# Feed-forward tiles from 4 on all by seven products, in three groups of six

## The chip, the cores and the metric

The kernel runs on one core of a Trainium2 chip. TensorE (PE in the profile, its weight loads PEld) multiplies, VectorE (DVE), ScalarE (ACT) and GpSimd (POOL) compute elementwise, and SyncE (SP) issues the DMA transfers. The metric is device time in microseconds (us), the median of several executions.

## The reference, cut to what matters

Two layers, each with a feed-forward before and after a mixer (a pooling mixer in the first layer, attention in the second). So the feed-forward runs four times, each time with its own weights:

```python
def swiglu(h, w_gate, w_up, w_down):
    return (jax.nn.silu(h @ w_gate) * (h @ w_up)) @ w_down

h = rmsnorm(x, ffn_norm)             # x: 512 tokens x 1024 channels, float32
x = x + 0.5 * swiglu(h, w_gate, w_up, w_down)   # 2816 hidden channels
```

## The kernel before, in words

All is kept transposed: channels on the 128 partitions, the 512 tokens along the free dimension. x lies in SBUF as eight tiles of 128x512 (`xs`). The 2816 hidden channels make 22 tiles of 128. Every factor of a product is split into a high part in a reduced format (ScalarE, L117) and the remainder, the low part (VectorE, L118); `mm3` then takes three matmuls in place of one: high x high, high x low, low x high.

A **plain** product of one tile (`product`, L264) is 8 blocks of x (k) times three matmuls, 24 matmuls of 512 columns. A **pair by seven products** (`Two`, L364) computes two tiles of the same weight matrix as a 2 x 2 block product: the two tiles, the two halves of the 1024 input channels and the two halves of the 512 tokens are the blocks, and Strassen's method (in Winograd's form) needs seven block products in place of eight. Each is 4 k x 3 matmuls of 256 columns, so a pair is 84 matmuls of 256 columns, where two plain products are 48 of 512. For this it needs sums of the weight blocks (`w_sums`, L335: two loads into `raw`, four additions on VectorE at L350, and splits of the two tiles and of the sums, 3.5 of 1024 columns), sums of the blocks of x (`x_sums`, L321: for each of four k four subtractions of 256 columns at L327 and two splits of 512), and additions that put the products together (L434, with copies by ScalarE at L391). The seven products of a pair, by number: 1 uses a11, 6 uses s2, 5 uses s1, 3 uses s4, 7 uses s3, 2 uses a12, 4 uses a22. `twos` (L401) interleaves the products of consecutive pairs; the first pair begins with 1, 7, 6, 2.

A feed-forward (`ffn_in`, L258) goes through three groups of hidden tiles, `THIRDS`, 0 to 8, 8 to 16 and 16 to 22. A group first makes its hidden tiles `hs`, then the **down stage** (L500) multiplies them with w_down: for each of the eight output blocks m it loads the group's part of w_down[m] (`load_w`, L125, three buffers each of `raw`, `whi`, `wlo`), takes three matmuls of 512 columns for each hidden tile, and adds half the sum to `xs[m]` (L511 on VectorE).

In the first group tiles 0 to 3 are plain for gate and up, since the normalised x isn't there yet: they use x times the gain and scale the result by the row factors afterwards (`scaled`, L276). Meanwhile `normed` makes the normalised x and its split. Tiles 4 to 7 of the first group have a plain up product each, with `x_sums` of k = 0 to 3 after them one by one, and two pairs for the gate (L477 to L491). In the two later groups gate and up are both done by pairs.

Buffers that the parts share: `slot` (39 tiles of 128x512) holds the splits of x, of the normalised x, of its sums, and the hidden tiles; `t` (10 tiles) takes what `slot` doesn't; `work` has 6; `s` holds the sums of the weights and, before, two of the normalised blocks that `x_sums` reads. Each engine executes its own queue in order. The compiler of the kernel orders the queues ahead of the run, so an instruction may stand ahead of one that comes earlier in the program.

Of the kernel before, what the change touches and what calls it, by code (L numbers as in the profile page):

```python
# [9 lines left out]
F32 = mybir.dt.float32  # L10
F32R = mybir.dt.float32r
I32 = mybir.dt.int32
BF16 = mybir.dt.bfloat16
AF = mybir.ActivationFunctionType
# [4 lines left out]
P = 128  # L19
D = 1024  # L20
S = 512
FF = 2816
KD = D // P
NT = S // P
NFT = FF // P
THIRDS = ((0, 8), (8, 16), (16, 22))
WINDOWS = (2, 4, 8, 16)
H = 8
DN, DR = 128, 64
# [48 lines left out]
def trunk(ctx: ExitStack, tc: tile.TileContext, a: dict, out: bass.AP):  # L78
    nc = tc.nc
# [17 lines left out]
        return sp.tile(shape or [P, S], F32R, tag="slot", name="slot")  # L97

    def work(shape=None):
        return kp.tile(shape or [P, S], F32, tag="work", name="work", bufs=6)  # L100

    def small(n, dt=F32, tag=None, bufs=3):
        return tp.tile([P, n], dt, tag=tag or f"sm{n}", name="small", bufs=bufs)
# [4 lines left out]
    def mm3(ps, w, x, first, last):  # L108

        mm(ps, w[0], x[0], first, False)  # L110
        mm(ps, w[0], x[1], False, False)
        mm(ps, w[1], x[0], False, last)
# [145 lines left out]
    def ffn_in(fp, wg, wu, wd, prep, nxt, first, final):  # L258
# [2 lines left out]
        KH = KD // 2  # L261
        rows = None

        def product(w, x, turned=False, then=None):  # L264

            hi, lo = load_w(w, WC)
            p = acc()
            for i in range(KD):
                if then and i == KD - 4:
                    then()  # L270
                k = i % 2 * KH + i // 2 if turned else i
                ks = slice(k * P, (k + 1) * P)
                mm3(p, (hi[:, ks], lo[:, ks]), x[k], i == 0, i == KD - 1)
            return p

        def scaled(p):  # L276
# [13 lines left out]
        def halved(z, zu):  # L290
            nc.vector.tensor_mul(z, z, zu)
            h = slot(), slot()
            split(z, *h)
            return h
# [6 lines left out]
        xn, ts, kept = [None] * KD, {}, []  # L301

        def extra():
            return fp.tile([P, S], F32R, tag="t", name="t", bufs=10)

        def normed(k):

# [13 lines left out]
        def x_sums(k):  # L321

            b12, b11, b22, b21 = (kept[k][:, c * C : (c + 1) * C] for c in range(4))
            t = [work(), work()]
            t1, t2, t3, t4 = (x[:, c * C : (c + 1) * C] for x in t for c in range(2))
            for out, x, y in ((t1, b12, b11), (t2, b22, t1), (t3, b22, b12), (t4, b21, t2)):
                nc.vector.tensor_tensor(out=out, in0=x, in1=y, op=ALU.subtract)  # L327
            for e in range(2):
                new = extra if k < 2 else slot
                hi, lo = new(), new()  # L330
                split(t[e], hi, lo)
                ts[k, 2 * e] = hi[:, :C], lo[:, :C]
                ts[k, 2 * e + 1] = hi[:, C:], lo[:, C:]

        def w_sums(top, low):  # L335

            hw = WC // 2
            rt = wp.tile([P, WC], F32, tag="raw", name="raw")
            rl = wp.tile([P, WC], F32, tag="raw", name="raw")
            nc.sync.dma_start(rt, top)  # L340
            nc.sync.dma_start(rl, low)
            a11, a12, a21, a22 = rt[:, :hw], rt[:, hw:], rl[:, :hw], rl[:, hw:]
            s12 = fp.tile([P, WC], F32, tag="s", name="s", bufs=2)
            s34 = fp.tile([P, WC], F32, tag="s", name="s", bufs=2)
            s1, s2, s3, s4 = s12[:, :hw], s12[:, hw:], s34[:, :hw], s34[:, hw:]
            for out, x, y, op in (
                (s1, a21, a22, ALU.add), (s2, s1, a11, ALU.subtract),
                (s3, a11, a21, ALU.subtract), (s4, a12, s2, ALU.subtract),
            ):
                nc.vector.tensor_tensor(out=out, in0=x, in1=y, op=op)  # L350

            def halves(pool, src, n, tag, bufs=None):
                hi = pool.tile([P, n], F32R, tag=tag + "hi", name="hi", bufs=bufs)
                lo = pool.tile([P, n], F32R, tag=tag + "lo", name="lo", bufs=bufs)
                split(src, hi, lo)
                return [(hi[:, c : c + hw], lo[:, c : c + hw]) for c in range(0, n, hw)]

            a11, a12 = halves(wp, rt, WC, "w")
            s1, s2 = halves(wp, s12, WC, "w")
            s3, s4 = halves(fp, s34, WC, "c", 2)  # L360
            (a22,) = halves(fp, a22, hw, "d", 1)
            return a11, a12, a22, s1, s2, s3, s4

        class Two:  # L364
# [36 lines left out]
        def twos(todo):  # L401

            last = None
            for two in (*todo, None):
                if two:
                    two.load()
                if not last or not two:
                    one = last or two
                    for n in (5, 4, 3) if last else (1, 7, 6, 2):
                        one.product(n)  # L410
                else:
                    for one, n in (
                        (last, 5), (two, 1), (last, 4), (two, 7), (two, 6), (last, 3), (two, 2)
                    ):
                        one.product(n)
                if last:
                    yield last
                last = two

        def silu(two):  # L420
            nc.scalar.activation(two.z[:, :C], two.r, AF.Silu)
            nc.scalar.activation(two.z[:, C:], two.z[:, C:], AF.Silu)
            return two.z
# [24 lines left out]
                        last and k == KH - 1 and e == 2, skip=True,  # L448
                    )

        for f0, f1 in THIRDS:
            hs = []
            for f in range(f0, min(f1, 4), 2):
                if first and f == 0:
                    pg, pu = opening(wg[0], wu[0], prep)
                else:
                    pg = product(wg[f], xh)
                    if f == 2:
                        normed(0)
                    pu = product(wu[f], xh)  # L460
                    if f == 2:
                        normed(1)
                if rows is None:
                    r = prep.rstd()
                qg = product(wg[f + 1], xh)
                if rows is None:
                    rows = prep.rstd_rows(r)
                zs = scaled(pg), scaled(pu)
                if f == 2:
                    normed(2)  # L470
                hs.append(gated([(slice(0, S), zs[0])], zs[1]))
                qu = product(wu[f + 1], xh)
                zs = scaled(qg), scaled(qu)
                if f == 2:
                    normed(3)
                hs.append(gated([(slice(0, S), zs[0])], zs[1]))
            if f0 == 0:  # L477
                us, zu = [], None
                for e in range(4, 8):
                    u = product(wu[e], xn, e == 4)  # L480
                    if e < 6:
                        zu = zu if zu is not None else fp.tile([P, 2 * S], F32, tag="z", name="z", bufs=3)
                        z = zu[:, (e - 4) * S : (e - 3) * S]
                        nc.scalar.activation(z, u, AF.Copy)
                        u = z
                    us.append(u)
                    x_sums(e - 4)
                for e, gate in enumerate(twos([Two(wg, 4), Two(wg, 6)])):
                    z = silu(gate)
                    for i, u in enumerate(us[2 * e : 2 * e + 2]):  # L490
                        hs.append(halved(z[:, i * S : (i + 1) * S], u))  # L491
            else:
                z = None
                for e, two in enumerate(twos([Two(w, f) for f in range(f0, f1, 2) for w in (wg, wu)])):
                    if e % 2 == 0:
                        z = silu(two)
                    else:
                        times(z, two)
            nf = f1 - f0
            for m in range(KD):  # L500
                hi, lo = load_w(wd[m][:, f0 * P : f1 * P], nf * P)

                nc_ = 2 if final and f1 == NFT and m == KD - 1 else 1
                for e in range(nc_):
                    p = acc()
                    cs = slice(e * S // nc_, (e + 1) * S // nc_)
                    for f in range(nf):
                        fs = slice(f * P, (f + 1) * P)
                        h = hs[f][0][:, cs], hs[f][1][:, cs]
                        mm3(p[:, cs], (hi[:, fs], lo[:, fs]), h, f == 0, f == nf - 1)  # L510
                    nc.vector.scalar_tensor_tensor(  # L511
                        out=xs[m][:, cs], in0=p[:, cs], scalar=0.5, in1=xs[m][:, cs],
                        op0=ALU.mult, op1=ALU.add,
                    )
                    if final and f1 == NFT:
                        nc.sync.dma_start(out[m][:, cs], xs[m][:, cs])
                if f1 == NFT and not final:
                    nxt.add(m)
# [669 lines left out]
```

## Time and profile before

| | |
|---|---|
| time, median of 3 runs (lowest to highest) | 1672.87 us (1672.41 to 1673.0) |
| profiled execution | 1674.59 us, span 1672.8 us |
| TensorE, matmuls | 99% busy, 10246 matmuls, granted clock 0.998 |
| TensorE, weight loads | 89% |
| VectorE | 71% |
| ScalarE | 48% |
| GpSimd | 4% |
| DMA | 161.69 MB, mean 97 GB/s |

The span is the time from the first to the last instruction of one profiled execution; the execution's own time has about 1.8 us around it. A busy share is a mean over the span; the windows further below split it by stage. The second feed-forward (the one that most rows are from) lies between about 377 and 736 us, the four layers are alike.

### The profile page before, as it was taken

What the parts mean: (1) busy time and instruction counts of PE and PEld (TensorE: products, weight loads), DVE (VectorE), ACT (ScalarE), POOL (GpSimd) and SP (SyncE); (2) the same over time, 40 slices, a digit from 0 to 9 for tenths busy, and PEclk for the clock granted to TensorE, in tenths of its full rate; (3) what the DMA queues carried; (4) which work ended last, traced back from release to release, by engine and by line L of the source; (5) the groups of instructions that cost most, each with busy time, mean ns of one, the idle gap of its engine ahead of it and who ended that gap; (6) DMA issues with size and microseconds to landing.
All of it is one profiled execution on the core that took longest, in us unless ns stands there. A gap on an engine that the chain in (4) does not pass through costs nothing.

```text
span 1672.8 us, 25532 instructions
## 1 busy us (share of the span) xinstructions
PE 1659.1 (99%) x10246; PEld 1491.9 (89%) x10246; DVE 1182.8 (71%) x1940; ACT 800.7 (48%) x1347; POOL 69.7 (4%) x147
## 2 busy tenths in 40 slices
PE   8999999999999999999999999999999999999999
PEld 7889989987889989988899899888888788899898
DVE  8847847798757757668568567656778786586673
ACT  6534524454534525545445345446665454354351
POOL 0000000011000000000000000003321300000000
PEclk9999999999999999999999999999999999999999
DMA  5333333332332332333323323321112123233332
GB/s 179 101 101 101 102 103 99 97 112 77 109 105 85 118 105 89 98 101 96 107 89 103 112 89 108 103 88 52 45 57 89 59 82 111 89 102 114 89 110 91
DMA packets 48215, 161.69 MB, mean 97 GB/s; under 512 B 5728, under 2 KB 6496, under 8 KB 48096
## 3 DMA queue, kind: packets, MB, share of 16 engines
q1 hardware_dynamic: 47520, 159.34, 30.9%
q8 instruction: 80, 1.31, 0.3%
q10 hardware_dynamic: 576, 0.72, 0.1%
q14 instruction: 39, 0.32, 0.1%
HBM read 157.94 MB, written 2.10 MB: 96 GB/s over the span
## 4 chain that ended last, share of the span: by engine, by line
PE 97%; DVE 2%; ACT 1%; issue 0%; DMA 0%; POOL 0%; ACTq 0%; DVEq 0%; POOLq 0%
PE acc L106 95%; PE aux L702 1%; PE aux L106 1%; DVE slot L121 1%; PE aux L983 0%; DVE x L1018 0%; DVE wlo L118 0%; ACT work L964 0%; DMA gains<-in_gains 0%; DVE x L576 0%; ACT slot L117 0%; ACT slot L120 0%; ACT whi L117 0%; POOL work L969 0%; ACT work L852 0%
## 5 line engine op out<-in xcount | busy, mean ns | idle before, releaser
L106 PE MATMUL acc<-slot,whi 128*128 128x512 f32 x2428 | 752.4, 391 | 8.4 <-ACT whi L117 5.1
L106 PEld LDWEIGHTS acc<-slot,whi 128*128 128x128 f32 x2428 | 454.9, 189 | 102.8 <-ACT whi L117 5.6
L106 PE MATMUL acc<-slot,wlo 128*128 128x512 f32 (+1 forms) x1206 | 470.6, 390 | 0.0
L106 PE MATMUL acc<-slot,hi 128*128 128x256 f32 x2304 | 424.6, 281 | 0.1
L106 PEld LDWEIGHTS acc<-slot,hi 128*128 128x128 f32 x2304 | 356.9, 189 | 2.9 <-DVE z L434 1.9
L117 ACT ACTIVATE whi<-raw 128x1024 fp32r<-128x1024 f32 (+2 forms) x181 | 179.8, 996 | 333.8 <-PE acc L106 261.4
L106 PE MATMUL acc<-slot,lo 128*128 128x256 f32 x1152 | 324.3, 282 | 0.0
L106 PEld LDWEIGHTS acc<-slot,wlo 128*128 128x128 f32 x1206 | 227.7, 189 | 48.0 <-DVE wlo L118 1.3
L118 DVE TENSOR_TENSOR wlo<-raw,whi 128x1024 fp32r<-128x1024 f32 (+2 forms) x180 | 208.2, 1158 | 86.1 <-ACT whi L117 84.9
L106 PE MATMUL acc<-t,hi 128*128 128x256 f32 x1280 | 242.9, 282 | 0.0
L106 PEld LDWEIGHTS acc<-slot,lo 128*128 128x128 f32 x1152 | 218.4, 190 | 0.0
L118 DVE TENSOR_TENSOR lo<-s,hi 128x1024 fp32r<-128x1024 f32 x128 | 156.3, 1224 | 75.7 <-ACT hi L117 75.6
L117 ACT ACTIVATE hi<-s 128x1024 fp32r<-128x1024 f32 x128 | 135.1, 1058 | 139.9 <-PE acc L106 89.4
L106 PEld LDWEIGHTS acc<-t,hi 128*128 128x128 f32 x1280 | 196.7, 189 | 0.0
L106 PE MATMUL acc<-t,lo 128*128 128x256 f32 x640 | 181.1, 283 | 0.0
L511 DVE SCALAR_TENSOR_TENSOR x<-acc,x 128x512 f32<-128x512 f32 (+1 forms) x97 | 66.3, 684 | 136.9 <-PE acc L106 136.9
L117 ACT ACTIVATE hi<-raw 128x512 fp32r<-128x512 f32 (+1 forms) x128 | 107.9, 843 | 83.6 <-PE acc L106 65.6
L350 DVE TENSOR_TENSOR s<-raw 128x512 f32<-128x512 f32 x128 | 85.7, 688 | 70.8 <-DMA raw<-in_ffn_gate 62.7
L391 ACT ACTIVATE m<-acc 128x256 f32<-128x256 f32 x192 | 73.0, 381 | 109.1 <-PE acc L106 108.6
L118 DVE TENSOR_TENSOR lo<-raw,hi 128x512 fp32r<-128x512 f32 (+1 forms) x128 | 121.0, 953 | 0.0
L106 PEld LDWEIGHTS acc<-t,lo 128*128 128x128 f32 x640 | 120.5, 188 | 0.0
L106 PE MATMUL acc<-whi,slot 128*128 128x384 f32 (+2 forms) x320 | 87.6, 344 | 0.0
(191 smaller groups left out, 1472.0 us busy)
## 6 DMA issues: line engine op xcount, KB each, us to landing
raw<-in_ffn_gate SPq DMA_DIRECT2D x87, 512.0 KB, 3.5
raw<-in_ffn_up SPq DMA_DIRECT2D x87, 512.0 KB, 3.6
raw<-in_ffn_down SPq DMA_DIRECT2D x64, 512.0 KB, 3.5
raw<-in_ffn_down SPq DMA_DIRECT2D x32, 384.0 KB, 3.5
raw<-in_w_q SPq DMA_DIRECT2D x12, 384.0 KB, 3.2
raw<-in_w_in SPq DMA_DIRECT2D x8, 512.0 KB, 3.5
raw<-in_w_out SPq DMA_DIRECT2D x8, 512.0 KB, 3.6
x<-in_xT SPq DMA_DIRECT2D x8, 256.0 KB, 5.2
```

Source lines behind the costliest of these rows:

```text
L106: nc.tensor.matmul(ps, lhsT, rhs, start=start, stop=stop, skip_group_check=skip)
L117: nc.scalar.activation(hi, src, AF.Copy)
L118: nc.vector.tensor_tensor(out=lo, in0=src, in1=hi.bitcast(F32), op=ALU.subtract)
L121: nc.vector.scalar_tensor_tensor(out=lo, in0=src, scalar=scale, in1=hi.bitcast(F32), op0=ALU.mult, op1=ALU.subtract)
L350: nc.vector.tensor_tensor(out=out, in0=x, in1=y, op=op)
L391: nc.scalar.activation(self.kept[:, c[(1, 6, 7).index(n)]], part, AF.Copy)
L511: nc.vector.scalar_tensor_tensor(out=xs[m][:, cs], in0=p[:, cs], scalar=0.5, in1=xs[m][:, cs], op0=ALU.mult, op1=ALU.add,)
L702: nc.tensor.transpose(p[:, i * P : (i + 1) * P], src(i), ident)
```

## The change

`THIRDS` becomes `CHUNKS`, four groups: tiles 0 to 3, all plain, with a down stage of their own, and three groups of six tiles, all by pairs for gate and up. The four plain up products of tiles 4 to 7 fall away, with their copies; two more pairs are computed in a layer (18 in place of 16). `x_sums` moves into the down loop of the first group, one k ahead of each odd output block m. `work` gets 7 buffers, `t` 6 (only the sums of k = 0 and one block of x use it), and the split of a22 two.

```diff
-THIRDS = ((0, 8), (8, 16), (16, 22))
+CHUNKS = ((0, 4), (4, 10), (10, 16), (16, 22))
...
-        return kp.tile(shape or [P, S], F32, tag="work", name="work", bufs=6)
+        return kp.tile(shape or [P, S], F32, tag="work", name="work", bufs=7)
...
-            return fp.tile([P, S], F32R, tag="t", name="t", bufs=10)
+            return fp.tile([P, S], F32R, tag="t", name="t", bufs=6)
...
-                new = extra if k < 2 else slot
+                new = extra if k == 0 else slot
...
-            (a22,) = halves(fp, a22, hw, "d", 1)
+            (a22,) = halves(fp, a22, hw, "d", 2)
...
-        for f0, f1 in THIRDS:
+        for f0, f1 in CHUNKS:
...
-            if f0 == 0:
-                us, zu = [], None
-                for e in range(4, 8):
-                    u = product(wu[e], xn, e == 4)
-                    if e < 6:
-                        zu = zu if zu is not None else fp.tile([P, 2 * S], F32, tag="z", name="z", bufs=3)
-                        z = zu[:, (e - 4) * S : (e - 3) * S]
-                        nc.scalar.activation(z, u, AF.Copy)
-                        u = z
-                    us.append(u)
-                    x_sums(e - 4)
-                for e, gate in enumerate(twos([Two(wg, 4), Two(wg, 6)])):
-                    z = silu(gate)
-                    for i, u in enumerate(us[2 * e : 2 * e + 2]):
-                        hs.append(halved(z[:, i * S : (i + 1) * S], u))
-            else:
+            if f0:
                 z = None
-                for e, two in enumerate(twos([Two(w, f) for f in range(f0, f1, 2) for w in (wg, wu)])):
+                todo = [Two(w, f) for f in range(f0, f1, 2) for w in (wg, wu)]
+                for e, two in enumerate(twos(todo)):
...
             for m in range(KD):
+                if f0 == 0 and m % 2:
+                    x_sums(m // 2)
                 hi, lo = load_w(wd[m][:, f0 * P : f1 * P], nf * P)
```

`product` also loses the arguments `turned` and `then`, which only these up products used.

## Rows read from the trace of the kernel before

**Rows 1.** The page: busy time by engine, and the chain that ended last.

```profile
PE 1659.1 (99%) x10246; PEld 1491.9 (89%) x10246; DVE 1182.8 (71%) x1940; ACT 800.7 (48%) x1347; POOL 69.7 (4%) x147
...
PE 97%; DVE 2%; ACT 1%; issue 0%; DMA 0%; POOL 0%; ACTq 0%; DVEq 0%; POOLq 0%
```

**Rows 2.** Windows: length, busy PE, PEld, DVE, ACT, POOL (instructions), granted clock, DMA.

```profile
445.52:466.50 20.98, 20.95 (x172) 20.47 (x171) 14.65 (x19) 12.08 (x18) 0.00 (x0) 1.00 0.40 119
...
509.34:589.33 79.99, 79.99 (x674) 79.98 (x672) 61.84 (x84) 44.66 (x68) 0.00 (x0) 1.00 0.33 102
589.33:632.86 43.53, 43.53 (x194) 36.05 (x193) 23.45 (x30) 11.18 (x12) 0.00 (x0) 1.00 0.34 105
```

**Rows 3.** Windows of the four plain up products, in three of the four layers.

```profile
53.80:75.69 21.89, 21.89 (x98) 18.02 (x96) 20.86 (x37) 11.59 (x17) 0.00 (x0) 1.00 0.23 73
423.65:445.52 21.87, 21.87 (x97) 18.01 (x96) 20.86 (x37) 11.59 (x17) 0.00 (x0) 1.00 0.23 73
...
1367.38:1389.25 21.87, 21.87 (x98) 18.01 (x97) 20.86 (x37) 11.59 (x17) 0.00 (x0) 1.00 0.24 72
```

**Rows 4.** TensorE's timeline at the end of the first group: start, duration, instructions.

```profile
464.10 0.63 PE L106 MATMUL acc<-slot,whi 128*128 128x512 f32 x2
464.56 0.39 PE L106 MATMUL acc<-slot,wlo 128*128 128x512 f32 x1
464.99 0.50 PE L106 MATMUL acc<-slot,hi 128*128 128x256 f32 x2
```

**Rows 5.** VectorE's timeline in the stretch 419 to 446.

```profile
419.31 1.23 DVE L118 TENSOR_TENSOR wlo<-raw,whi 128x1024 fp32r<-128x1024 f32 x1
423.84 0.69 DVE L278 TENSOR_TENSOR work<-acc,rows 128x512 f32<-128x512 f32 x1 [3.30 <-PE acc L106]
...
426.38 0.69 DVE L118 TENSOR_TENSOR slot<-work,slot 128x512 fp32r<-128x512 f32 x1
...
428.86 0.42 DVE L327 TENSOR_TENSOR work<-s 128x256 f32<-128x256 f32 x1
429.19 0.42 DVE L327 TENSOR_TENSOR work<-s,work 128x256 f32<-128x256 f32 x1
...
439.68 0.69 DVE L350 TENSOR_TENSOR s<-raw 128x512 f32<-128x512 f32 x1
440.28 0.69 DVE L350 TENSOR_TENSOR s<-raw,s 128x512 f32<-128x512 f32 x1
440.88 1.22 DVE L118 TENSOR_TENSOR lo<-raw,hi 128x1024 fp32r<-128x1024 f32 x1
442.02 2.36 DVE L118 TENSOR_TENSOR lo<-s,hi 128x1024 fp32r<-128x1024 f32 x2
444.29 0.69 DVE L118 TENSOR_TENSOR lo<-raw,hi 128x512 fp32r<-128x512 f32 x1
```

**Rows 6.** VectorE's timeline in the first group's down stage.

```profile
493.73 0.69 DVE L350 TENSOR_TENSOR s<-raw 128x512 f32<-128x512 f32 x1 [3.86 <-DMA raw<-in_ffn_gate]
494.34 0.68 DVE L511 SCALAR_TENSOR_TENSOR x<-acc,x 128x512 f32<-128x512 f32 x1
```

**Rows 7.** The page's DMA issues: instructions, KB each, us to landing.

```profile
raw<-in_ffn_down SPq DMA_DIRECT2D x64, 512.0 KB, 3.5
raw<-in_ffn_down SPq DMA_DIRECT2D x32, 384.0 KB, 3.5
```

**Rows 8.** Windows and timeline between the attention layer and the last feed-forward.

```profile
1319.30:1321.70 2.40, 0.32 (x2) 0.00 (x0) 2.40 (x2) 1.39 (x3) 2.32 (x2) 1.00 0.00 0
1321.70:1328.55 6.85, 6.14 (x14) 4.80 (x15) 4.19 (x4) 0.19 (x1) 1.70 (x2) 0.50 0.46 153
1170.00:1190.00 20.00, 19.06 (x119) 16.49 (x118) 17.07 (x50) 14.60 (x43) 3.42 (x10) 1.00 0.25 73
...
1319.23 0.39 PE L106 MATMUL acc<-slot,whi 128*128 128x512 f32 x1
...
1322.41 0.80 PE L106 MATMUL acc<-slot,whi 128*128 128x512 f32 x1 [2.79 <-DVE slot L121]
```

More of the change, by code (lines that the diff above doesn't have):

```diff
@@ L262, in ffn_in, with product @@
         rows = None
-        def product(w, x, turned=False, then=None):
+        def product(w, x):
             hi, lo = load_w(w, WC)
@@ L268, in product @@
             for i in range(KD):
[L269 to L273, printed above, removed]
+                ks = slice(i * P, (i + 1) * P)
+                mm3(p, (hi[:, ks], lo[:, ks]), x[i], i == 0, i == KD - 1)
             return p
```

## The prediction

> **What bounds the kernel now.** I read the page's busy shares and its chain of waits first. TensorE is busy 99% of the span and holds 97% of the chain; VectorE, at 71%, holds 2% [rows 1]. So what a change is worth is matmul time saved minus gaps made. The clock is at its upper level (2.4 GHz) wherever a feed-forward layer runs. Next the windows by stage of the second feed-forward layer show how evenly TensorE runs [rows 2]: a stage of eight seven-product tiles (672 matmuls of 256 columns) takes 79.99 us, 0.1190 us a matmul, and a down stage of eight tiles (192 matmuls of 512 columns) takes 43.53 us, 0.2267 us a matmul. TensorE is never idle in either. VectorE is not evenly loaded, though: 61.84 of 79.99 us in the seven-product stage, 23.45 of 43.53 in the down stage, but 20.86 of 21.87 us in the window 423.65 to 445.52, where the four plain up products run; the four layers agree in this to 0.01 us, and three of them stand in the rows [rows 3]. That 95% is the place to watch, because the change puts more VectorE work into just this stretch.
>
> **What it saves on TensorE.** Per layer four plain up products go (4 x 24 matmuls of 512 columns) and two pairs by seven products come (2 x 84 of 256). Two plain products cost 48 x 0.2267 = 10.88 us, a pair 84 x 0.1190 = 10.00 us: 0.88 us less for a pair, 1.77 us a layer, 7.1 us in four layers. The down matmuls stay 22 tiles x 24, only cut 4+6+6+6 instead of 8+8+6. By the Trainium skill ("TensorE: Matmul & The Clock Gate", section "Back-to-back issue gap") a matmul at the full clock takes N/2.4 plus about 2.5 ns, which makes 109 and 216 ns and a saving of about 9.5 us in all (an estimate from that page); the rows have 119 and 227 ns, so I take the 7.1.
>
> A small loss goes too. In the old first group the last pair has nobody behind it, and TensorE waits for VectorE's addition into z: from 464.56 to 464.99 it needs 0.43 us for a step of 0.23 [rows 4]. The window 445.52 to 466.50 holds 168 short and 3 long matmuls, 19.99 + 0.68 = 20.67 us, and took 20.98: 0.31 us a layer. The groups that stay have no such loss in rows 2, so I count it as gained. Together the change can win at most 4 x (1.77 + 0.31) = 8.3 us.
>
> **What it puts on VectorE.** The stretch that begins when the last plain product (up, tile 3) ends, at 423.65, is 21.8 us long both ways: before, four up products, 96 x 0.2267; after, the first down stage, 8 x 12 x 0.2267 = 21.76 us. Then TensorE goes on to the first seven-product pair. In that time VectorE has to finish tile 3, make the sums of x (moved from between the up products into the down loop), and make the weight sums of the first pair. Starts behind one another [rows 5]: a 128x512 operation 0.60 us (439.68 to 440.28), 128x256 0.335 (428.86 to 429.19), 128x1024 1.135 (440.88 to 442.02).
> - Before: scaling 0.60; four x_sums of 4 x 0.335 + 2 x 0.60 = 2.54, 10.16; tile 3's product and low half 1.20; two up splits 2.27 (the other two were done earlier, the last at 419.31); weight sums and splits 4 x 0.60 + 3 x 1.135 + 0.60 = 6.41. Sum 20.6 us; the rows go from 423.84 to 444.98, 21.1 us, so 0.5 us is lost. It just fits.
> - After: the two splits of 1024 columns (2.27) become six of 512 (3.60; the first two of eight are done ahead, as now), and seven additions into x of 0.60 (4.20) come in, the eighth being free to come later. 20.6 - 2.27 + 3.60 + 4.20 + 0.5 = 26.7 us. VectorE is done at 450.5, and TensorE wants to start at 423.65 + 21.76 = 445.4.
>
> The pair's first block needs only the first split; the second block needs a sum of w, hi and low, at the third matmul: 445.4 + 1.43 + 0.24 = 447.1. The split of a22 is last (0.60) and needed later still, so s3, s4 are ready at 449.9 and s1, s2 at 448.8. If the block on s2 comes second the stall is 1.7 us, if the one on s3 does, 2.8 us. From below: VectorE idles 3.30 us before 423.84, waiting for TensorE; the kernel puts nothing in there, though the first sum of x had its data by then, but two shorter splits make room of 1.1 us in the queue, and a whole x_sums moved up would take 2.54 us off: the stall could be nothing. (That the order of an engine's queue departs from the program is to be seen: the weight sum of the next group, L350 at 493.73, stands ahead of an L511 that the program has earlier [rows 6].) From above: the eighth addition put in front (0.60) and the 0.5 us lost twice make 3.9 us. I take **1.8 us**: the s2 order without moving up, or the s3 order with 1 us moved up. It comes once a layer: a pair takes VectorE 61.84/8 = 7.7 us with its share of the gate products, TensorE 10.0, so the lag is worked off within the next pair.
>
> **What I cost at nothing.** ScalarE has 11.59 of 21.87 us in the stretch [rows 3]; it gets eight splits of half the length in place of four and loses two copies of u, so it stays under two thirds. GpSimd has no work there (0.00 in rows 3). SyncE's queue: the sums of x issue no transfer; the same bytes of w_down come in 32 loads a layer instead of 24. A load of 512 KB lands in 3.5 us, one of 384 KB also in 3.5 [rows 7]; the first group's are 256 KB, every 2.72 us, with three buffers (8 us), so they are in time. If that cover were gone, each load could cost up to 0.8 us. The first pair's loads wait for raw buffers freed by the last splits of w_down, some 5 us ahead of use. Eight more additions into x a layer (0.60 each) lie in down stages, which have 20 us of VectorE to spare [rows 2]. The down stage of a group of six follows its last pair with four finished tiles, 4 x 3 x 0.2267 = 2.7 us of cover for the last one; the group of six before does the same. In the first group tile 3 has three tiles ahead, 2.0 us, for a chain of scaling, product and two halves of about 3 us (423.84 to 427.07); TensorE can begin the next output block meanwhile, and the time would lie within the VectorE lag anyway. The larger pools (work, d) and the smaller t cost no instruction.
>
> **Sum.** 4 x (1.77 + 0.31 - 1.8) = 1.1 us less. The profiled execution had 1674.59 us (span 1672.8 and 1.8 around it); 1673.5 after the change. The three timed runs have a median of 1672.87, so the same 1.1 us off gives **1671.8 us**. A measurement here can tell 0.2%, 3.3 us, from no change; a stall between 1.25 and 2.9 us a layer stays within it.
>
> **The rivals.**
> - *The stall is covered* (sums of x move up into VectorE's idle 3.3 us, or the order of blocks hides it): stall 0 to 1.2 us a layer, 4 to 8.3 us faster, 1664.6 to 1669. For it: the idle time is there in all four layers, and the data are. Against it: with the same data the kernel before leaves it empty.
> - *VectorE's queue is ordered badly* (an addition into x, which waits for TensorE, stands ahead of a split or of the weight sums): the lag grows beyond 2.9 us, to 3.9 and more, 4 x (3.9 - 2.08) = 7 us slower, 1680. It decides from 2.9 us on. For it: VectorE executes in queue order, and eight such waits are mixed into a full stretch; against it, with 26 us of work there is nearly always an addition whose block is already done.
> - *The stall takes the clock*: before 1322.41 TensorE had waited 2.79 us in one piece (behind a matmul at 1319.23), and from 1321.70 to 1328.55 it was granted 0.50, the lower level, 1.2 GHz; such a stretch gives 3.4 us less work [rows 8]. If a stall of 2.8 us in one piece does it in each layer: 4 x (2.8 + 3.4 - 2.08) = 16 us slower, 1689. It decides only if the wait is in one piece of that size; from 1170 to 1190, with 0.94 us of idle time in all, the clock stayed at 1.00, so what a wait between these sizes does is open. The Trainium skill (same page, "HAM oscillation") says that idle gaps send the clock back and that every following burst then starts slow; rows 8 agree for one gap.
>
> **How the numbers follow.** Forecast (within 3.3 us of no change) 0.38; covered 0.34; badly ordered 0.18; clock 0.10. So faster 0.34, same 0.38, slower 0.28. The range runs from no stall, 1664.5, to a stall of 4.2 us without the clock, 1681; the clock and what is left of bad order are outside. The forecast's own range is 1669.5 to 1676.2.
>
> **What would show it.** Right: the 256-column stages at 0.119 us a matmul; VectorE above 95% in the first down stage of each layer; one wait of TensorE of 1 to 3 us for L118 (low halves of sums) at the first pair; no others. The sums of x among the eight down blocks. Wrong: a feed-forward layer without gaps (then 1664.6), gaps at later pairs, gaps at the down stage's start, or a granted clock of 0.5 inside a feed-forward layer.

## The result, and the profile after

The changed kernel takes 1683.18 us (median; 1682.52 to 1683.65), the kernel before beside it 1672.93: ratio 1.0061, 95% interval 1.0049 to 1.0074. It is slower by 10.25 us. Forecast were 1671.8 and no change that could be told, and the range ended at 1681. The profiled execution had 1683.58 us, span 1681.7.

Windows by stage of the changed kernel, columns as in [rows 2]. The first four are the first stage of pairs (six pairs, 504 matmuls) in the four layers; then a later stage of pairs and a down stage of six tiles; last the first down stage of the second layer, the stretch of [rows 3]:

```profile
75.71:139.29 63.58, 60.99 (x506) 60.17 (x505) 51.97 (x72) 34.73 (x53) 0.00 (x0) 1.00 0.33 105
447.25:512.11 64.86, 62.24 (x506) 61.46 (x505) 52.09 (x72) 34.73 (x53) 0.00 (x0) 0.97 0.31 103
797.57:862.47 64.90, 62.25 (x505) 61.64 (x504) 52.13 (x72) 34.73 (x53) 0.00 (x0) 0.97 0.31 103
1395.33:1460.30 64.97, 62.23 (x506) 61.61 (x504) 52.21 (x73) 34.76 (x53) 0.00 (x0) 0.97 0.31 103
544.75:604.73 59.98, 59.98 (x506) 59.98 (x505) 44.84 (x62) 32.50 (x50) 0.00 (x0) 1.00 0.30 93
512.11:544.75 32.64, 32.64 (x147) 27.04 (x146) 20.45 (x28) 9.61 (x12) 0.00 (x0) 1.00 0.41 119
425.30:447.25 21.95, 21.95 (x97) 17.85 (x96) 21.46 (x42) 10.64 (x17) 0.00 (x0) 1.00 0.37 109
```

The later stages keep the old pace, 59.98/504 = 0.1190 us and 32.64/144 = 0.2267 us a matmul. The loss is in the first stage of pairs alone, against 504 x 0.1190 = 59.98 us: 3.6 us in the first layer, 4.9 to 5.0 in each of the others, 18.4 in all. Less the 4 x 2.08 us expected as gain that is +10.1 us, close to the measured 10.25. (The spans of the two profiled executions differ by 8.9 only. The one before lay 1.7 us above its median, and it had a stretch at half clock between attention and the last layer [rows 8] that this one didn't have.)

TensorE's timeline at the first pair of the second layer; in brackets the idle time ahead and what ended it:

```profile
448.56 0.28 PE L106 MATMUL acc<-slot,lo 128*128 128x256 f32 x1
450.26 0.50 PE L106 MATMUL acc<-t,hi 128*128 128x256 f32 x2 [1.42 <-ACT hi L117]
451.96 0.58 PE L106 MATMUL acc<-t,lo 128*128 128x256 f32 x1 [1.20 <-DVE lo L118]
```

The first block is done, the second waits for the high half of a sum of weights and then for its low half. At the old pace its third matmul, the first to read the low half, would start at 447.25 + 1.43 + 0.24 = 448.92 (twelve matmuls of the first block and two of the second); it starts at 451.96, 3.0 us later. VectorE's queue over the same time, to be held against [rows 5] (L274 was L278, L346 was L350, L495 was L511):

```profile
420.71 0.68 DVE L118 TENSOR_TENSOR wlo<-raw,whi 128x512 fp32r<-128x512 f32 x1
425.47 0.69 DVE L274 TENSOR_TENSOR work<-acc,rows 128x512 f32<-128x512 f32 x1 [4.08 <-PE acc L106]
...
444.74 1.22 DVE L118 TENSOR_TENSOR lo<-raw,hi 128x1024 fp32r<-128x1024 f32 x1
...
447.08 0.68 DVE L346 TENSOR_TENSOR s<-raw 128x512 f32<-128x512 f32 x1
447.68 0.68 DVE L495 SCALAR_TENSOR_TENSOR x<-acc,x 128x512 f32<-128x512 f32 x1
448.28 0.68 DVE L346 TENSOR_TENSOR s<-s,raw 128x512 f32<-128x512 f32 x1
448.88 0.68 DVE L346 TENSOR_TENSOR s<-raw 128x512 f32<-128x512 f32 x1
449.49 0.68 DVE L346 TENSOR_TENSOR s<-raw,s 128x512 f32<-128x512 f32 x1
450.09 0.68 DVE L118 TENSOR_TENSOR lo<-raw,hi 128x512 fp32r<-128x512 f32 x1
450.69 1.21 DVE L118 TENSOR_TENSOR lo<-s,hi 128x1024 fp32r<-128x1024 f32 x1
```

VectorE is idle for 4.08 us before 425.47 and then works almost without a pause (21.46 of the 21.95 us in the last window above). Before, the four weight sums were made between 437 and 441, some 5 us ahead of use; now the last is at 449.49, behind TensorE's need. The eighth addition into x (447.68) and the split of a22 (450.09) both stand ahead of the low half that TensorE waits for (450.69). ScalarE makes the high half of the sum only at 449.16, as soon as the sum is there. The weights themselves had landed before that: the last split of them by ScalarE, first line, starts at 444.98, and the first sum is made at 447.08.

```profile
444.98 0.63 ACT L117 ACTIVATE hi<-raw 128x512 fp32r<-128x512 f32 x1 [0.34 <-DMA raw<-in_ffn_gate]
...
448.88 0.38 ACT L387 ACTIVATE m<-acc 128x256 f32<-128x256 f32 x1 [3.27 <-PE acc L106]
449.16 1.05 ACT L117 ACTIVATE hi<-s 128x1024 fp32r<-128x1024 f32 x1
```

This high half was begun before the last sum, s4, was made (449.49), so it is that of s1 and s2. The block that waits is thus product 6, on s2: TensorE takes the first pair in the order 1, 6 where the program has 1, 7, 6.

In the first layer the same two waits make TensorE 3.0 us late. Another 0.5 us of its 3.6 stands behind two weight loads that wait for ScalarE's copy of a block's sum (L387 above), each idle for 0.21 us and worth 0.27 us of the matmuls' pace:

```profile
82.55 0.30 PEld L106 LDWEIGHTS acc<-t,hi 128*128 128x128 f32 x2 [0.21 <-ACT m L387]
...
84.83 0.30 PEld L106 LDWEIGHTS acc<-slot,hi 128*128 128x128 f32 x2 [0.21 <-ACT m L387]
```

And at the end of the wait the clock falls. Windows at the wait in the first layer, then in the second from 0.5 us before the wait's end; the granted clock is the third number from the end:

```profile
77.00:82.00 5.00, 2.41 (x18) 2.00 (x17) 5.00 (x7) 3.22 (x4) 0.00 (x0) 1.00 0.46 145
...
451.44:454.86 3.42, 2.90 (x13) 2.90 (x14) 3.42 (x5) 0.66 (x1) 0.00 (x0) 0.50 0.75 298
```

In the second, third and fourth layers 3.41 us run at the lower level, 1.2 GHz; in the first the same wait (1.42 and 1.17 us) left it at the upper one.

### The profile page after: what moved, and what is told of

Same layout as the page of the kernel before. It is cut to its first block, busy times and chain, and to the rows that moved or that the text cites. A ratio compares the mean times of both kernels' runs of the same rounds, so it can differ in the third digit from the quotient of the medians.

```text
span 1681.7 us, 26443 instructions
## 1 busy us (share of the span) xinstructions
PE 1656.5 (99%) x10534; PEld 1502.5 (89%) x10534; DVE 1242.9 (74%) x2068; ACT 823.8 (49%) x1411; POOL 70.0 (4%) x147
## 5 line engine op out<-in xcount | busy, mean ns | idle before, releaser
L106 PE MATMUL acc<-slot,hi 128*128 128x256 f32 x3168 | 585.4, 283 | 0.0
L106 PEld LDWEIGHTS acc<-slot,hi 128*128 128x128 f32 x3168 | 494.3, 191 | 1.8 <-ACT m L387 0.8
L106 PE MATMUL acc<-slot,lo 128*128 128x256 f32 x1584 | 448.0, 283 | 0.0
L106 PE MATMUL acc<-slot,wlo 128*128 128x512 f32 x1094 | 425.1, 389 | 0.0
L117 ACT ACTIVATE whi<-raw 128x768 fp32r<-128x768 f32 (+2 forms) x197 | 169.4, 862 | 310.1 <-PE acc L106 223.0
L106 PEld LDWEIGHTS acc<-slot,lo 128*128 128x128 f32 x1584 | 301.4, 190 | 0.0
L118 DVE TENSOR_TENSOR wlo<-raw,whi 128x768 fp32r<-128x768 f32 (+2 forms) x196 | 193.3, 988 | 106.4 <-ACT whi L117 103.9
L495 DVE SCALAR_TENSOR_TENSOR x<-acc,x 128x512 f32<-128x512 f32 x129 | 88.2, 684 | 126.8 <-PE acc L106 126.2
L117 ACT ACTIVATE hi<-raw 128x1024 fp32r<-128x1024 f32 (+1 forms) x144 | 121.5, 845 | 123.2 <-PE acc L106 72.6
L387 ACT ACTIVATE m<-acc 128x256 f32<-128x256 f32 x216 | 82.5, 382 | 145.5 <-PE acc L106 145.5
L118 DVE TENSOR_TENSOR lo<-raw,hi 128x1024 fp32r<-128x1024 f32 (+1 forms) x144 | 136.3, 949 | 0.3 <-ACT hi L117 0.2
L346 DVE TENSOR_TENSOR s<-raw 128x512 f32<-128x512 f32 x144 | 96.1, 685 | 10.4 <-DMA raw<-in_ffn_up 8.9
```

Of the source, the lines that this page charges most:

```text
L106: nc.tensor.matmul(ps, lhsT, rhs, start=start, stop=stop, skip_group_check=skip)
L117: nc.scalar.activation(hi, src, AF.Copy)
L118: nc.vector.tensor_tensor(out=lo, in0=src, in1=hi.bitcast(F32), op=ALU.subtract)
L387: nc.scalar.activation(self.kept[:, c[(1, 6, 7).index(n)]], part, AF.Copy)
L495: nc.vector.scalar_tensor_tensor(out=xs[m][:, cs], in0=p[:, cs], scalar=0.5, in1=xs[m][:, cs], op0=ALU.mult, op1=ALU.add,)
```

## The experiments

The question was whether the amount of VectorE's work makes the wait (theory A), or the chain load, sum, halves (theory B), or the sums' place in the program (theory C), and what the clock adds (theory K). Times are medians; ratios are to the kernel before, run beside each. The kernels of the first four runs stood beside 1673.58 us, those of the last four beside 1672.96.

**Sums of x for k = 0 earlier.** Tile 3's scaling of the gate product, `normed(3)`, then the sums, then the scaling that waits:

```diff
+EARLY = 1
...
-                zs = scaled(qg), scaled(qu)
+                zg = scaled(qg)
                 if f == 2:
                     normed(3)
+                    for k in range(EARLY):
+                        x_sums(k)
+                zs = zg, scaled(qu)
...
-                if f0 == 0 and m % 2:
+                if f0 == 0 and m % 2 and m // 2 >= EARLY:
```

> The changed kernel, with one edit: the sums of x for k = 0 are issued with tile 3's normalisation, ahead of the scaling that waits for the last plain product, so that they can run in VectorE's idle time there (4.08 us in the changed kernel). Theory A (VectorE has more work in the first down stage than the stage is long, 26.8 us against 21.8, and the first pair waits for the rest): 2.54 us of the work leave the full stretch, TensorE's wait at the first pair falls from 3.2 to about 0.7 us in each layer, the clock no longer falls inside a feed-forward layer; 4 x 2.5 + 3 x 1.5 less, about 1669 us, faster than the kernel before the change. Theory B (the wait comes from the chain load, sum, high half, low half of the first pair's weights, each on the other's heels, not from the amount of VectorE's work): the wait stays at 3 us and the time at 1683.

Measured 1667.38 us, ratio 0.9958 (0.9942 to 0.9975): faster than both kernels, 6.2 us under the one before. VectorE's queue (line numbers are one higher in this kernel) has the sums in the idle time, of which 1.35 us is left:

```profile
416.70 0.75 DVE L324 TENSOR_TENSOR work<-s 128x256 f32<-128x256 f32 x2
...
418.64 1.48 DVE L119 TENSOR_TENSOR t<-work,t 128x512 fp32r<-128x512 f32 x2
421.46 0.69 DVE L275 TENSOR_TENSOR work<-acc,rows 128x512 f32<-128x512 f32 x1 [1.35 <-PE acc L107]
```

The first stages of pairs lose 0.3 and 0.9 us in the first two layers (0.6 and 0.3 in the others, with 60.53 and 60.25 us), and the clock stays up:

```profile
75.08:135.33 60.25, 60.25 (x505) 60.09 (x504) 49.38 (x68) 33.58 (x52) 0.00 (x0) 1.00 0.35 111
443.27:504.16 60.89, 60.45 (x506) 60.12 (x505) 50.13 (x69) 33.82 (x52) 0.00 (x0) 1.00 0.34 110
```

The blocks, loads and groups are the same; 2.54 us of VectorE's work in another place take away 3.3 to 4.7 us a layer, the clock's part included. Theory B falls as the cause of this wait.

**No sums of x at all.**

```diff
-                if f0 == 0 and m % 2:
-                    x_sums(m // 2)
...
-            return lambda k: ts[k, i]
+            return lambda k: [t[:, i % 2 * C : (i % 2 + 1) * C] for t in xn[i // 2 * KH + k]]
```

> The changed kernel without the sums of x: the blocks that should read them read blocks of the normalised x of the same size, so all matmuls are done. 10.2 us of VectorE's work leave the stretch. Theory A: no wait at the first pair, 1664.6 us (1672.9 less 4 x 2.08). Theory B: with VectorE free, the first pair's sums still come late behind their loads, a wait of 1 us or more stays, 1669 or above.

Measured 1666.25 us, ratio 0.9953 (0.9938 to 0.9968). The first stages take 60.24 to 60.32 us, so 0.3 us a layer is lost with VectorE free. It isn't theory B's wait either: what TensorE waits for is ScalarE's copy of the first block's sum, second view, ahead of a block that adds to the same sum. The time is about the bound for any placing of the sums, and the kernel above is near it.

```profile
74.95:135.27 60.32, 60.32 (x506) 60.01 (x504) 49.03 (x68) 33.19 (x52) 0.00 (x0) 1.00 0.36 111
```

```profile
77.02 0.30 PEld L106 LDWEIGHTS acc<-slot,hi 128*128 128x128 f32 x2 [0.21 <-ACT m L387]
```

**The kernel before, with more VectorE work.**

```diff
                     x_sums(e - 4)
+                    for _ in range(2):
+                        q = work()
+                        nc.vector.tensor_tensor(out=q, in0=rows, in1=rows, op=ALU.add)
```

> The kernel before the change, with eight more additions of 128x512 a layer on VectorE (two after each up product's sums of x, their result used by nobody): 4.8 us more in the stretch that had 1.0 us to spare, about as much as the change brings in there. Theory A: the first pair's low halves, done 2 to 3 us ahead of need before, come 2 us late; a wait of about 2 us at the first pair of each layer, 1681 us without and 1685 with a fall of the clock. Theory B (something in the new grouping itself): 1673, no change.

Measured 1678.89 us, ratio 1.0029 (1.0018 to 1.0039): 5.3 us slower, in the old grouping. TensorE now waits at the first pair there:

```profile
449.26 0.51 PE L106 MATMUL acc<-t,hi 128*128 128x256 f32 x2 [0.48 <-ACT hi L117]
```

In the second layer the stage's first 156 matmuls take 19.90 us in place of 156 x 0.1190 = 18.57: 1.3 us, where 2 were expected; the clock didn't fall. The amount of work does it, without the new grouping.

```profile
446.85:466.75 19.90, 19.33 (x158) 18.72 (x156) 15.97 (x21) 11.97 (x19) 0.00 (x0) 1.00 0.40 133
```

**Sums of x ahead of the first four output blocks.**

```diff
-                if f0 == 0 and m % 2:
-                    x_sums(m // 2)
+                if f0 == 0 and m < 4:
+                    x_sums(m)
```

> The changed kernel with the sums of x issued ahead of the output blocks m = 0 to 3 in place of m = 1, 3, 5, 7: the same work in the same stretch, earlier in the queue. Theory A: the queue is full either way, so TensorE waits as long in all (3 to 3.5 us a layer), now partly inside the down stage for splits of w_down; without the fall of the clock 1679, with it 1683. Theory C (the sums stand too late in the program, at m = 7 just ahead of the first pair): the wait goes, 1668 to 1670.

Measured 1690.63 us, ratio 1.0097 (1.0082 to 1.0112). This is worse than either theory had it. The sums now stand ahead of a split of w_down that TensorE needs; TensorE's timeline and VectorE's:

```profile
437.51 0.50 PE L106 MATMUL acc<-slot,wlo 128*128 128x512 f32 x1 [3.14 <-DVE wlo L118]
```

```profile
436.43 0.42 DVE L323 TENSOR_TENSOR work<-chi,work 128x256 f32<-128x256 f32 x1
436.77 0.68 DVE L118 TENSOR_TENSOR wlo<-raw,whi 128x512 fp32r<-128x512 f32 x1
...
445.52 0.69 DVE L495 SCALAR_TENSOR_TENSOR x<-acc,x 128x512 f32<-128x512 f32 x1 [0.70 <-PE acc L106]
...
449.42 0.69 DVE L346 TENSOR_TENSOR s<-raw 128x512 f32<-128x512 f32 x1 [2.60 <-DMA raw<-in_ffn_gate]
```

The first stage of pairs still loses 1.5 us (61.50 in the second layer). So theory C falls, and my own "as long in all" too: the wait that came early isn't all given back later, because VectorE in turn then waits 0.70 us for TensorE, ahead of an addition, and 2.60 us for the weights of the first pair (last two lines). Place matters beside amount, but inside the full stretch this one only moved the wait forward; ahead of the stretch it helps.

**A filler for TensorE.**

```diff
                         one.product(n)
+                        if n == 1 and f0 == 4:
+                            spare = aux()[:, :C]
+                            for _ in range(18):
+                                mm(spare, one.products[1][1][0][:, :P], xn[0][0][:, :C], True, True)
```

> The changed kernel, with 18 more matmuls of 256 columns a layer (2.1 us, their sums read by nobody) on TensorE behind the first pair's first block, where TensorE waits for 3.2 us in pieces. Theory K (1.5 us a layer of the loss is the clock, which fell to 0.50 for 3.41 us behind this wait in three of four layers): the matmuls lie in the wait, the wait that is left is about 1 us, the clock stays at 1.00 and the first stages of all layers take 63.5 us instead of 63.6 to 65.0; 4 to 5 us less than the changed kernel, 1679. Theory A alone (only the wait counts): no change, 1683, or 2 us a layer more if the matmuls don't fit into the wait.

Measured 1680.88 us, ratio 1.0050 (1.0036 to 1.0063). By the time alone it isn't told apart from the changed kernel (1.0049 to 1.0074). By the profiled executions it is (1679.59 us against 1683.58): the first stages of pairs take 63.5 to 63.8 us in all four layers, with 2.1 us of extra matmuls in them, and the clock stayed up:

```profile
75.91:139.73 63.82, 62.90 (x524) 62.29 (x522) 52.29 (x73) 34.81 (x53) 0.00 (x0) 1.00 0.32 105
447.45:510.95 63.50, 62.90 (x524) 62.29 (x522) 51.87 (x72) 34.80 (x53) 0.00 (x0) 1.00 0.33 105
```

So in the profiled execution of the changed kernel the first stage loses some 3.6 us a layer by waiting, and the clock's fall costs 1.3 to 1.4 us more in each layer in which it comes.

**Two operations less ahead of the sums' halves.**

```diff
-            (a22,) = halves(fp, a22, hw, "d", 2)
+            a22 = a12 if lean else halves(fp, a22, hw, "d", 2)[0]
...
+                self.lean = f == 4 and w is wg
...
+                    if f0 == 0 and m == KD - 1:
+                        continue
                     nc.vector.scalar_tensor_tensor(
                         out=xs[m][:, cs], in0=p[:, cs], scalar=0.5, in1=xs[m][:, cs],
```

> The changed kernel without two of VectorE's operations a layer that stand ahead of the first pair's split sums: the addition of the first group's last output block into x (left out), and the split of the first pair's a22 (its block is multiplied with a12 instead). If their place in the queue, 0.6 us each, is the step that the prediction had wrong, TensorE's wait falls from 3.2 to about 2.0 us a layer; with the clock at 1.00 then 1672.5, with its fall in each layer 1678. If the wait comes from something ahead of them it stays at 3 us and the time at 1683.

Measured 1679.65 us, ratio 1.0038 (1.0025 to 1.0050). In the fourth layer, the one in which the clock stayed up, the first stage of pairs takes 62.82 us:

```profile
1394.44:1457.26 62.82, 60.52 (x505) 60.11 (x504) 51.23 (x70) 34.65 (x53) 0.00 (x0) 1.00 0.35 106
```

That is 2.8 us lost where the changed kernel loses 3.6 in its one layer with the clock up, the first: the two operations count 0.8 us, not 1.2. With them gone VectorE itself waits for ScalarE, first line, and TensorE waits in one piece for the high half, second:

```profile
449.98 2.36 DVE L118 TENSOR_TENSOR lo<-s,hi 128x1024 fp32r<-128x1024 f32 x2 [0.48 <-ACT hi L117]
```

```profile
450.95 0.78 PE L106 MATMUL acc<-t,hi 128*128 128x256 f32 x4 [2.40 <-ACT hi L117]
```

**Sums of x for k = 0 and 1 earlier**, as in the first experiment but with `EARLY = 2`, and the pools of the kernel before.

> The sums of x for k = 0 and k = 1 both ahead of the scaling that waits for the last plain product, with the pools of the kernel before (t 10, work 6, one buffer for the split of a22). VectorE has 4.08 us idle there and the two sums take 5.1 us. Theory A: the wait of 0.3 to 0.9 us that is left with one sum moved goes to nothing, and tile 3 comes 1 us later, hidden by the next output blocks: 1665 to 1666. If tile 3's lateness isn't hidden, 1 us a layer more than with one: 1671.

Measured 1666.10 us, ratio 0.9961 (0.9949 to 0.9974), as good as one sum moved, and not told apart from it. Three first stages lose 0.3 us, the third layer 1.8 (61.81 us). There VectorE waits 2.66 us for the first pair's weights, in the second layer 0.97; why that load took longer, the runs don't say.

```profile
438.00 1.29 DVE L347 TENSOR_TENSOR s<-raw 128x512 f32<-128x512 f32 x2 [0.97 <-DMA raw<-in_ffn_gate]
...
785.56 1.29 DVE L347 TENSOR_TENSOR s<-raw 128x512 f32<-128x512 f32 x2 [2.66 <-DMA raw<-in_ffn_gate]
```

**The subtractions on GpSimd.**

```diff
-                nc.vector.tensor_tensor(out=out, in0=x, in1=y, op=ALU.subtract)
+                nc.gpsimd.tensor_tensor(out=out, in0=x, in1=y, op=ALU.subtract)
```

> The changed kernel with the 16 subtractions of 256 columns a layer of the sums of x on GpSimd in place of VectorE. 5.4 us leave VectorE's queue. If the two engines don't hinder each other, the wait at the first pair goes to nothing, 1665 to 1667. In the kernel before, VectorE's operations of 0.74 us took up to 1.75 us beside GpSimd's additions between attention and the last feed-forward; if that holds here, GpSimd's some 13 us in the stretch make VectorE 5 to 13 us slower, and the time is 1683 to 1710.

Measured 1676.01 us, ratio 1.0021 (1.0012 to 1.0030): between the two guesses. GpSimd did take work off, some of it ahead of the stretch, but VectorE's 512-column operations take up to 1.23 us beside it in place of 0.68 (three in 3.51 us beside GpSimd, first line, and two in 1.28 later):

```profile
426.87 2.31 POOL L323 TENSOR_TENSOR work<-chi,work 128x256 f32<-128x256 f32 x2
...
427.38 3.51 DVE L118 TENSOR_TENSOR slot<-work,slot 128x512 fp32r<-128x512 f32 x3
...
436.21 1.28 DVE L118 TENSOR_TENSOR slot<-work,slot 128x512 fp32r<-128x512 f32 x2
...
442.56 0.69 DVE L346 TENSOR_TENSOR s<-raw 128x512 f32<-128x512 f32 x1 [2.67 <-DMA raw<-in_ffn_gate]
```

There the first pair's sums wait for a load (last row), so with the queue half empty theory B's chain comes up as the next thing in the way. How much of the remaining loss is the load and how much GpSimd, no run separates.

## Why the prediction was wrong

- *The gain*, 2.08 us a layer, was right: the pace of both kinds of matmul is unchanged, and without the sums of x the kernel is 7.3 us faster than before (bound 8.3). What is missing is the 0.3 us a layer that TensorE waits for ScalarE's copy, for which the prediction had no term.
- *The place and the amount* were right: VectorE's queue is 98% full in the first down stage, and the wait is at the first pair, for the sums of the weights. The amount alone makes a wait in the old grouping (+4.8 us of work, 1.3 us lost), and the wait goes when the work goes or moves ahead.
- *The step that failed is "I take 1.8 us", and in it two operations put behind the one that is waited for: "the eighth being free to come later" and "the split of a22 is last".* The block on s2 came second, and nothing was moved up into the idle time (it grew from 3.30 to 4.08 us); for just this case the sum gave 1.7 us. But the low half of s1 and s2 is there at 451.90, 26.6 us after the stretch began at 425.30, where the sum had 448.8 - 423.65 = 25.15. Of these 1.45 us, 1.2 are the eighth addition (447.68) and the split of a22 (450.09), 0.60 each, which stand ahead of it. So TensorE's third matmul was 3.0 us late and not 1.7.
- *ScalarE* was costed at nothing by its load, and its place in the chain left out. Without the two operations only 0.8 us came back, since VectorE then waits 0.48 us for the high half, which takes 1.05 us on ScalarE between sum and low half. The 0.6 us between 3.0 and the 3.6 that the first layer's stage loses are the two waits for ScalarE's copy, 0.27 each with the restart, and 0.1 at the restart behind the low half.
- That 3.6 lies near the upper end that I had worked out, 3.9, is chance: that end took the block on s3 as the second.
- *The clock* had a chance of 0.10 and a condition, 2.8 us in one piece. It fell in three layers of four at a wait in two pieces of 1.4 and 1.2 us, so the condition was wrong. The price, 3.4 us by rows 8, was too high: the lower level lasted 3.41 us here and not 6.85, and cost 1.35. 4 x (3.6 - 2.08) = 6.1 us, and 3 x 1.35 for the clock, make 10.1; 10.25 were measured. Without the clock the time, some 1679, would have been inside the range; the range left the clock out.
- *The rival "covered"* was the kernel that should have been written: the data for the first sum were there, the room too, but the queue took the sum ahead only where the program did (1667.38 us). The rival "badly ordered" was nearest: slower by 7 us from a lag of 3.9, by an addition that stands ahead; but that addition takes its 0.60 us of the queue, and didn't wait for TensorE there.
- The rest that I cost at nothing held: no wait at the first down stage's start, loads of 256 KB landing in 2.7 us, later groups of six without a gap.

## What to carry to other kernels

Where one engine is the bound on the whole, look for the short stretch in which another is full, and add up that engine's queue through to the operation that the bound engine waits for, with everything that stands ahead of it and the other engine's hop in between. A wait on TensorE costs more than itself if the clock falls at its end: here 1.35 us on top of some 3. Work whose inputs are early belongs in the idle time ahead of a wait, and the program has to put it there: the same change with one sum of x moved up is 0.4% faster than before in place of 0.6% slower.

## What was not expected of the hardware

A wait doesn't decide the clock by its length. In the run with the sums first, TensorE waited 3.1 to 3.2 us in each layer; the clock fell behind it in two layers and not in the others. Windows of that run, from the end of the wait on, in the second layer and in the fourth:

```profile
437.51:440.92 3.41, 2.84 (x11) 2.06 (x12) 3.41 (x8) 1.53 (x4) 0.00 (x0) 1.00 0.27 77
...
1388.10:1391.52 3.42, 3.42 (x9) 2.68 (x10) 3.42 (x8) 1.26 (x2) 0.00 (x0) 0.50 0.29 81
```

In the run with two operations less, waits of 2.2 to 2.4 us in one piece lowered it in three layers, and one of 2.3 us in the fourth didn't. Between attention and the last feed-forward TensorE waits 2.8 us in all ten profiled executions; the clock fell there in six, the kernel before among them [rows 8], and not in the other four, the changed kernel among them:

```profile
1330.17 0.50 PE L106 MATMUL acc<-slot,whi 128*128 128x512 f32 x1 [2.81 <-DVE slot L121]
```

```profile
1330.20:1340.00 9.80, 9.01 (x43) 7.27 (x43) 5.02 (x6) 2.12 (x2) 1.06 (x1) 1.00 0.49 140
```

In the runs in which no wait in a feed-forward layer was longer than 1.02 us, it never fell there. And GpSimd beside VectorE nearly doubles VectorE's time for a 512-column operation with both inputs in SBUF, 0.68 to 1.23 us.
